# Eight experts on one core: the chunks of the two kinds of expert issued as a pipeline

## The chip, the cores and the metric

The kernel runs on one core of a Trainium2 chip. TensorE (PE) multiplies, VectorE (DVE) and ScalarE (ACT) do the elementwise work, and SyncE (SP) issues nearly all transfers from HBM. The metric is the device time of one execution in microseconds; lower is better.

## The reference

A two-layer latent-diffusion backbone over 256 latent tokens and 256 context tokens of width 1024. Each layer is a modulated norm, one input projection split over four mixers, an output projection, and a channel mixer. The channel mixer of the second layer, the part that the change touches, is top-2 of 8 SwiGLU experts:

```python
def moe_swiglu(h, router, w1, w3, w2):
    logits = (h @ router).astype(jnp.float32)
    top_v, top_i = lax.top_k(logits, TOP_K)
    probs = jax.nn.softmax(top_v, axis=-1)
    combine = jnp.sum(jax.nn.one_hot(top_i, N_EXPERTS, dtype=jnp.float32) * probs[..., None], axis=-2).astype(h.dtype)
    out = jnp.zeros_like(h)
    for e in range(N_EXPERTS):
        out = out + combine[..., e:e + 1] * swiglu(h, w1[e], w3[e], w2[e])
    return out
```

Each expert has w1 and w3 of 1024 x 3584 and w2 of 3584 x 1024, all in float32: 44 MB an expert, 352 MB for the eight.

## The kernel before

**Tiling.** Everything up to the router takes the first half of the run; then come the experts, in `moe`. The kernel sorts the eight experts by load. Three are *heavy* (up to 128 tokens each) and five are *light* (up to 64 tokens). An expert's 3584 inner columns are cut into seven *chunks* of 512. A chunk needs six *units* of weights of 1 MB each: two of w1, two of w3, two of w2.

**A heavy chunk** works in two float32r parts for each operand. Each unit is *split*: ACT rounds a half to float32r (line 145), DVE takes the rest (line 146), and the raw buffer is then free. `moe_first` multiplies by w1 and w3 (three products for each block of 128 rows, lines 176, 181, 182), takes Silu of the first on ACT and multiplies by the second on DVE. `moe_second` *turns* the rows g on PE (transposes, line 1104), copies them into G1 and G2 (lines 1107, 1108), and multiplies by w2 into the two banks `y0`, `y1`.

**A light chunk** multiplies the raw float32 weights as they land, two products side by side in the array. `light_first` is line 1139 (with Silu in 1144 and the multiply in 1145), `light_second` turns the rows (1153, 1155) and multiplies by w2 into `yl` (1163).

**Order.** `moe` makes one list of (expert, chunk) steps: four light chunks first, then both kinds interleaved evenly. A step does the first products of its chunk and then the turning and the second products of the chunk *before* it, of whatever kind that was. After an expert's last chunk, `scatter` or `light_scatter` scales its result, turns it back to tokens and adds it to the residual (`put`, lines 1187 to 1190). The tokens of later experts are gathered in steps (line 1058) between the weight units of the chunks, one step a unit.

**What sets the order on the engines.** A scheduler orders each engine's instructions by priority on a modelled timeline; `keep` pins an instruction behind the one issued before it on its engine. The products of the experts are pinned, the transposes that turn the rows are not. Loads and splits carry a high priority (`ahead`), so they are issued as early as their buffers allow.

**Buffers.** Ten raw buffers of 1 MB are used in turn by both kinds (`load_raw`, line 119), and four halves each for the two split parts, which is two units. Three further buffers serve once at the start, and four units of the first light chunk lie in the split buffers that no heavy chunk uses yet.

Of the kernel before, what the change touches and what calls it, by code (L numbers as in the profile page):

```python
# [9 lines left out]
F32 = mybir.dt.float32  # L10
# [3 lines left out]
AF = mybir.ActivationFunctionType  # L14
ALU = mybir.AluOpType
# [7 lines left out]
EFF_CH = 7  # L23
NE = 8


NH, CAP, LCAP = 3, 128, 64
# [22 lines left out]
class Net:  # L50
# [1028 lines left out]
    def pt_tile(self):  # L1079
        return self.E.tile([128, 2, 128], F32R, tag="PT", name=self.nm("PT"), bufs=2)  # L1080

    def moe_first(self, src, XE, c, aside=lambda: None):

        nc = self.nc
        hs = []
        for name in ("m_w1", "m_w3"):
            ps = self.bank(tag="mm")
            for kh in range(2):
                w = self.split_unit(src(name, c, kh))
                for kk in range(4):  # L1090
                    k = 4 * kh + kk
                    self.mm3(ps, (XE[:, 0, k], XE[:, 1, k]), w(512 * kk, 512 * kk + 512), k == 0, k == 7)
                aside()
            hs.append(ps)
        g = self.t2()
        nc.scalar.activation(g, hs[0], AF.Silu)
        nc.vector.tensor_tensor(g, g, hs[1], op=ALU.mult)
        return g

    def moe_second(self, src, c, g, y, last=False):  # L1100
        nc, E = self.nc, self.E
        pt = self.bank((128, 4, 128), tag="sm")
        for j in range(4):
            nc.tensor.transpose(pt[:, j], g[:, 128 * j:128 * j + 128], self.ident)  # L1104
        G1 = E.tile([128, 4, 128], F32R, tag="G1", name=self.nm("G1"), bufs=2)
        G2 = E.tile([128, 4, 128], F32R, tag="G2", name=self.nm("G2"), bufs=2)
        nc.scalar.copy(G1, pt)  # L1107
        nc.vector.tensor_tensor(G2, pt, G1.bitcast(F32), op=ALU.subtract)
        for hb in range(2):
            self.cut = 2 if last and hb + self.ncut > 1 else 1  # L1110
            w = self.split_unit(src("m_w2", c, hb))
            self.cut = 1
            for b in range(2):
                j = 2 * hb + b
                for hf in range(2):
                    o = 1024 * b + 512 * hf
                    self.mm3(y[hf], (G1[:, j], G2[:, j]), w(o, o + 512), c == 0 and j == 0, c == EFF_CH - 1 and j == 3)

    def raw_unit(self, src):
        if self.halves:  # L1120
# [3 lines left out]
            raw = self.load_raw(src)  # L1124
        return lambda a, b: raw[:, a:b]

    def light_first(self, src, XL, c, aside=lambda: None):

        nc = self.nc
        hs = []  # L1130
        for name in ("m_w1", "m_w3"):
            ps = self.bank((128, 256), tag="mm")
            for kh in range(2):
                w = self.raw_unit(src(name, c, kh))
                for kk in range(4):
                    k = 4 * kh + kk
                    for b in range(2):
                        o = 512 * kk + 256 * b
                        self.keep(nc.tensor.matmul(ps[64 * b:64 * b + 64], XL[:, k], w(o, o + 256), start=(k == 0),  # L1139
                                                   stop=(k == 7), tile_position=(0, 64 * b)))  # L1140
                aside()
            hs.append(ps)
        g = self.t2()[:, :256]
        nc.scalar.activation(g, hs[0], AF.Silu)
        nc.vector.tensor_tensor(g, g, hs[1], op=ALU.mult)  # L1145
        return g

    def light_second(self, src, c, g, y, last=False):

        nc, E = self.nc, self.E  # L1150
        pt = self.bank((128, 2, 128), tag="sm")
        for j in range(2):
            nc.tensor.transpose(pt[:, j], g[:, 128 * j:128 * j + 128], self.ident)  # L1153
        G = E.tile([128, 2, 128], F32, tag="GL", name=self.nm("GL"), bufs=2)
        nc.scalar.copy(G, pt)  # L1155
        for hb in range(2):
            self.cut = 2 if last and hb + self.ncut > 1 else 1
            w = self.raw_unit(src("m_w2", c, hb))
            self.cut = 1
            for b in range(2):  # L1160
                for hf in range(2):
                    o = 1024 * b + 512 * hf
                    self.keep(nc.tensor.matmul(y[64 * hf:64 * hf + 64], G[:, b, 64 * hb:64 * hb + 64], w(o, o + 512),  # L1163
                                               start=(c == 0 and hb == b == 0), stop=(c == EFF_CH - 1 and hb == b == 1),
                                               tile_position=(0, 64 * hf)))

    def scatter(self, PT, y, cmb):

# [39 lines left out]

    def moe(self):
        nc, E = self.nc, self.E  # L1210
        XE, PT = {}, {}

        def tables(i):
            tabs = (self.pos, self.sel, self.comb) if i == 0 else self.placed
# [19 lines left out]
        def turn(i, P, Q=None):  # L1234
            if Q is None:
                self.turned(PT[i], [P[:, t, :128] for t in range(2)])
            else:
                self.turned(PT[i].rearrange("p t h c -> p (t h) c"), [x for t in range(2) for x in (P[:, t, 128:], Q[:, t])])

        def gather(i, j):  # L1240

            P = E.tile([128, 2, 256], F32R, tag="P", name=self.nm("P"), bufs=1)
            if i:
                heavy(i, P)
            Q = light(j, P)
            yield from self.gather(P[:, :, 0 if i else 128:192], XE.get(i), XE[j])
            if i:
                turn(i, P)
            turn(j, P, Q)

        def begin():
            yield from gather(None, 0)
            self.weights()
            self.by_load()
            yield
            yield from gather(1, NH + 1)

        def run(gen, n=1000):
            for _ in range(n):
                if next(gen, self) is self:  # L1260
                    break

        big = lambda i: 0 < i <= NH
        pend, side, late = None, begin(), iter(())
        run(side, 9)
        hs, ls = ([(i, c) for i in p for c in range(EFF_CH)] for p in (range(1, NH + 1), [0, *range(NH + 1, NE)]))

        n = self.lead
        rest = [((k + 0.5) / len(q), x) for q in (hs, ls[n:]) for k, x in enumerate(q)]
        steps = ls[:n] + [x for _, x in sorted(rest, key=lambda a: a[0])]  # L1270
        more = {(NH + k, 2): (k + 1 if k < NH else None, NH + k + 1) for k in range(1, NE - NH - 1)}
        y = {}
        for i, c in steps:
            e = self.ids[i]
            if i == 0:
                src = lambda name, c, j: self.d[name][0, c, j]
            else:
                src = lambda name, c, j, e=e: self.d[name][bass.ds(e, 1), c, j].rearrange("a p c -> (a p) c")
            if i == 0 and c == 4:
                self.gdma = False  # L1280
                gf = self.O.tile([128, 2, 1024], F32, tag="gf", name="gf")
                self.g2, self.fg = self.gate(2, 0, gf[:, 0]), gf[:, 1]
                nc.scalar.dma_start(self.fg, self.d["fng"])
            if c == 0 and i not in PT:
                run(side)
            g = (self.moe_first if big(i) else self.light_first)(src, XE[i], c, lambda: run(side, self.gstep))
            run(late)
            if pend is not None:
                late = self.moe_finish(*pend, PT, tables)
                run(late, 1)  # L1290
            if c == 0:
                y[big(i)] = self.ys() if big(i) else self.bank(tag="yl")
            pend = (i, src, c, g, y[big(i)])
            if (i, c) in more:
                run(side)
                side = gather(*more[i, c])
        run(late)
        run(self.moe_finish(*pend, PT, tables))

    def moe_finish(self, i, src, c, g, y, PT, tables):  # L1300
        last = i == NE - 1 and c == EFF_CH - 1
        big = 0 < i <= NH
        (self.moe_second if big else self.light_second)(src, c, g, y, last)
        if c == EFF_CH - 1:
            yield from (self.scatter if big else self.light_scatter)(PT[i], y, tables(i)[2])

    def moe_rest(self):

        nc, E, V = self.nc, self.E, self.nc.vector
# [4 lines left out]
        with self.tc.If(over > 0):  # L1314
            with self.tc.For_i(0, NE, 1) as e:
# [3 lines left out]
                for name, a in (("pos", self.pos[:, :2]), ("sel", self.sel), ("comb", self.comb),  # L1319
                                ("slots", self.slots)):  # L1320
                    q = self.tmp
# [8 lines left out]
                XE, PT = self.xe_tile(), self.pt_tile()  # L1330
# [3 lines left out]
                src = lambda name, c, i: self.d[name][bass.ds(e, 1), c, i].rearrange("a p c -> (a p) c")  # L1334
                y = self.ys()
                for c in range(EFF_CH):
                    g = self.moe_first(src, XE, c)
                    self.moe_second(src, c, g, y)
                for _ in self.scatter(PT, y, cmb):
                    pass  # L1340
                V.tensor_scalar(cur, cur, -1.0, None, op0=ALU.add)
# [318 lines left out]
```

## Time and profile before

| | |
|---|---|
| median of 3 runs | 1692.35 us (1692.28 to 1695.18) |
| profiled execution | 1697.85 us, its span 1696.1 us |
| granted TensorE clock, mean | 0.984 |
| PE busy | 1624.5 us, 96% of the span |
| weight loads on PE | 1187.7 us, 70% |
| DVE / ACT busy | 961.3 us, 57% / 685.0 us, 40% |
| HBM read | 478.86 MB |

A busy share is an average over stages with different limits, and matmuls are pipelined, so a busy PE is not a PE at its peak. The experts' weights are moved from 795 us to about 1664 us of the span; that stretch is the one to read. The profiled execution is 5.5 us longer than the median of the timed runs.

### The profile page before, as it was taken

To read this page: it belongs to the slowest core of one execution; us is meant where nothing else is said; L and a number is where in the kernel's file an instruction comes from. 1 tells how busy PE (TensorE), PEld (TensorE's weight loads), DVE (VectorE), ACT (ScalarE), POOL (GpSimd) and SP (SyncE) were. 2 spreads that over 40 slices of the span, in tenths; PEclk is the share of its full clock that TensorE was granted. 3 is DMA by queue.
4 is the path that set the end of the run, shared out by engine and by line. 5 is a ranking of instruction groups with operands and counts; after the bars stand their busy time and mean duration, and the time that the engine had idled before them with its cause. 6 is when DMAs were issued, how large, how long until landed. Compare 5 with 4: busy or idle time off the path is not lost. (4 is left out here: it accounts for less than half of the span.)

```text
span 1696.1 us, 23693 instructions
## 1 busy us (share of the span) xinstructions
PE 1624.5 (96%) x9333; PEld 1187.7 (70%) x9333; DVE 961.3 (57%) x1455; ACT 685.0 (40%) x1086; POOL 35.4 (2%) x46
## 2 busy tenths in 40 slices
PE   6999999999999999999899999999999999999996
PEld 3878799887787878999656566656665666665663
DVE  3769655568565688588424454446463535363354
ACT  4654244422222226665424334334453343343342
POOL 1000000000000031000000000000000000000000
PEclk8999999999999999999799999999999999999998
DMA  8544451444443542325799999999999999999993
GB/s 348 196 174 147 154 190 51 174 148 177 163 183 127 203 167 101 125 76 203 312 394 420 419 419 410 384 413 400 420 415 415 420 406 387 411 419 419 420 419 132
DMA packets 69031, 481.56 MB, mean 284 GB/s; under 512 B 8064, under 2 KB 8192, under 8 KB 12336
## 3 DMA queue, kind: packets, MB, share of 16 engines
q1 hardware_dynamic: 68480, 479.43, 71.5%
q8 instruction: 75, 1.23, 0.3%
q10 hardware_dynamic: 432, 0.54, 0.1%
q14 instruction: 44, 0.36, 0.1%
HBM read 478.86 MB, written 1.08 MB: 283 GB/s over the span
## 5 line engine op out<-in xcount | busy, mean ns | idle before, releaser
L146 DVE TENSOR_TENSOR s<-raw,s 128x1024 fp32r<-128x1024 f32 (+1 forms) x376 | 446.4, 1222 | 134.9 <-ACT s L145 134.4
L145 ACT CAST s<-raw 128x1024 fp32r<-128x1024 f32 (+1 forms) x376 | 383.1, 1049 | 270.2 <-PE mm L182 109.3
L176 PE MATMUL mm<-X,s 128*128 128x512 f32 (+1 forms) x672 | 247.4, 369 | 0.0
L181 PE MATMUL mm<-X,s 128*128 128x512 f32 (+1 forms) x672 | 247.3, 368 | 0.0
L182 PE MATMUL mm<-X,s 128*128 128x512 f32 (+1 forms) x672 | 246.0, 368 | 0.0
L1139 PE MATMUL mm<-raw,XL 128*64 128x256 f32 x1808 | 207.5, 381 | 0.0
L1139 PEld LDWEIGHTS mm<-raw,XL 128*64 128x64 f32 x1808 | 127.2, 137 | 71.2 <-issue 12.2
L176 PEld LDWEIGHTS mm<-X,s 128*128 128x128 f32 x672 | 126.6, 188 | 27.7 <-issue 6.7
L181 PEld LDWEIGHTS mm<-X,s 128*128 128x128 f32 x672 | 126.9, 189 | 25.8 <-issue 5.9
L182 PEld LDWEIGHTS mm<-X,s 128*128 128x128 f32 x672 | 126.7, 189 | 23.9 <-issue 3.4
L181 PE MATMUL mm<-s,XE 128*128 128x512 f32 x336 | 138.3, 411 | 4.2 <-DVE s L146 4.2
L176 PE MATMUL mm<-s,XE 128*128 128x512 f32 x336 | 135.7, 404 | 3.0 <-ACT s L145 3.0
L182 PE MATMUL mm<-s,XE 128*128 128x512 f32 x336 | 134.7, 401 | 0.0
L1163 PE MATMUL yl<-raw,GL 128*64 128x512 f32 x456 | 110.3, 604 | 1.0 <-ACT GL L1155 1.0
L1145 DVE TENSOR_TENSOR t<-t,mm 128x256 f32<-128x256 f32 x35 | 14.7, 421 | 170.2 <-PE mm L1139 170.2
L181 PEld LDWEIGHTS mm<-s,XE 128*128 128x128 f32 x336 | 64.4, 192 | 36.4 <-issue 13.8
L176 PE MATMUL mm<-s,X 128*128 128x256 f32 (+1 forms) x304 | 87.3, 289 | 2.0 <-ACT mix L666 2.0
L181 PE MATMUL mm<-s,X 128*128 128x256 f32 (+1 forms) x304 | 86.8, 287 | 0.8 <-DVE s L146 0.8
L182 PE MATMUL mm<-s,X 128*128 128x256 f32 (+1 forms) x304 | 86.0, 288 | 0.0
L176 PEld LDWEIGHTS mm<-s,XE 128*128 128x128 f32 x336 | 64.4, 192 | 23.9 <-ACT s L145 7.5
L181 PE MATMUL y<-s,G 128*128 128x512 f32 x168 | 68.8, 410 | 11.3 <-DVE s L146 11.3
L1107 ACT CAST G<-sm 128x512 fp32r<-128x512 f32 x21 | 12.3, 586 | 160.0 <-PE sm L1104 160.0
(382 smaller groups left out, 2273.9 us busy)
## 6 DMA issues: line engine op xcount, KB each, us to landing
raw<-in_m_w_dram SPq DMA_DIRECT2D x294, 1024.0 KB, 10.0
mraw<-in_mod_w_dram SPq DMA_DIRECT2D x47, 1024.0 KB, 4.8
raw<-in_f_w_dram SPq DMA_DIRECT2D x33, 1024.0 KB, 4.9
mraw<-in_m_w_dram SPq DMA_DIRECT2D x32, 1024.0 KB, 9.8
raw<-in_w_in_dram SPq DMA_DIRECT2D x20, 1024.0 KB, 4.8
raw<-in_w_out_dram SPq DMA_DIRECT2D x8, 1024.0 KB, 5.5
first<-in_m_w_dram SPq DMA_DIRECT2D x8, 512.0 KB, 8.7
once<-in_m_w_dram SPq DMA_DIRECT2D x3, 1024.0 KB, 16.2
```

What stands on the lines that cost most here:

```text
L145: self.last = (nc.scalar.copy(s1[:, :h], r), nc.vector.tensor_tensor(s2[:, :h], r, s1[:, :h].bitcast(F32), op=ALU.subtract))
L146: nc.vector.tensor_tensor(s2[:, :h], r, s1[:, :h].bitcast(F32), op=ALU.subtract))
L176: m = mm(out, a[0], b[0], start=first, stop=False)
L181: self.keep(mm(out, a[0], b[1], start=False, stop=False))
L182: self.keep(mm(out, a[1], b[0], start=False, stop=last))
L1107: nc.scalar.copy(G1, pt)
L1139: self.keep(nc.tensor.matmul(ps[64 * b:64 * b + 64], XL[:, k], w(o, o + 256), start=(k == 0), stop=(k == 7), tile_position=(0, 64 * b)))
L1145: nc.vector.tensor_tensor(g, g, hs[1], op=ALU.mult)
L1163: self.keep(nc.tensor.matmul(y[64 * hf:64 * hf + 64], G[:, b, 64 * hb:64 * hb + 64], w(o, o + 512), start=(c == 0 and hb == b == 0), stop= ...
```

## The change

The products are the same and so are all transfers. What changes is the order in which the steps' parts are issued:

- `moe_second` and `light_second` lose their turning, which becomes `moe_turn` and `light_turn`. Their transposes are now pinned too.
- Light rows are turned after the first product (w1) of the next step, heavy rows at the start of the next heavy step.
- The second products of a heavy chunk are issued between the two first products (w1 and w3) of the next heavy chunk; those of a light chunk ahead of a later light step, or behind it where the next step is light again.
- A light step that is followed by a heavy one loads and splits the heavy chunk's two w1 units (`self.pre`) ahead of its own multiply on DVE, which is pinned behind those splits.
- Gather steps run only in heavy steps, three at a time in three of the four places, and whatever is left runs just before the expert's first step. The gather for the first heavy expert, which ran between the units of the first light chunks, now runs behind the fifth.
- The heavy chunks are drawn forward by a factor of 0.95 in the list, so that the list ends heavy, light, light; before it ended light, heavy, light. The last heavy expert's second products and its scatter now come ahead of the last light chunk.

```diff
     def moe_first(self, src, XE, c, aside=lambda n: None):
...
+        g = self.t2()
+        for n, name in enumerate(("m_w1", "m_w3")):
             ps = self.bank(tag="mm")
             for kh in range(2):
...
+                if n == kh == 1:
+                    nc.vector.tensor_tensor(g, g, ps, op=ALU.mult)
+                elif kh == 1:
+                    nc.scalar.activation(g, ps, AF.Silu)
+                aside(2 * n + kh)
...
+    def moe_turn(self, g):
+
         nc, E = self.nc, self.E
         pt = self.bank((128, 4, 128), tag="sm")
         for j in range(4):
-            nc.tensor.transpose(pt[:, j], g[:, 128 * j:128 * j + 128], self.ident)
+            self.keep(nc.tensor.transpose(pt[:, j], g[:, 128 * j:128 * j + 128], self.ident))
         G1 = E.tile([128, 4, 128], F32R, tag="G1", name=self.nm("G1"), bufs=2)
         G2 = E.tile([128, 4, 128], F32R, tag="G2", name=self.nm("G2"), bufs=2)
         nc.scalar.copy(G1, pt)
         nc.vector.tensor_tensor(G2, pt, G1.bitcast(F32), op=ALU.subtract)
+        return G1, G2
...
+                aside(2 * n + kh)
+            if n == 0:
+                nc.scalar.activation(g, ps, AF.Silu)
+            else:
+                self.keep(nc.vector.tensor_tensor(g, g, ps, op=ALU.mult))
         return g
...
-        rest = [((k + 0.5) / len(q), x) for q in (hs, ls[n:]) for k, x in enumerate(q)]
+        rest = [((k + 0.5) / len(q) * f, x) for q, f in ((hs, 0.95), (ls[n:], 1)) for k, x in enumerate(q)]
...
+        def heavy_aside(n):
+            if n == 1:
+                turns(False)
+                puts()
+                second(True)
             else:
+                run(side, 3)
...
+            def light_aside(n):
+                if n == 1:
+                    turns(False)
+                if n == 3 and big(after[0]):
+
+                    if after[0] not in ready:
+                        puts()
+                        run(side)
+                    src = source(after[0])
+                    self.pre = [self.split_unit(src("m_w1", after[1], kh)) for kh in range(2)]
+
+            if kind:
+                turns(True)
+                g[i, c] = self.moe_first(source(i), XE[i], c, heavy_aside)
+            else:
+                second(False)
+                g[i, c] = self.light_first(source(i), XE[i], c, light_aside)
+                if not big(after[0]):
+                    second(False)
+            todo[kind].append((i, c))
+            if not kind and todo[True] and not any(big(x) for x, _ in steps[m:]):
+                turns(True)
+                second(True, aside=lambda: turns(False))
+                puts()
...
+        turns(False)
+        second(False, last=True)
+        puts()
```

## Rows read from the trace of the kernel before

**Rows 1.** The page: GB/s moved in 40 slices of 42.4 us.
```profile
GB/s 348 196 174 147 154 190 51 174 148 177 163 183 127 203 167 101 125 76 203 312 394 420 419 419 410 384 413 400 420 415 415 420 406 387 411 419 419 420 419 132
```

**Rows 2.** Windows by stage: busy us of each engine, PE clock, DMA share, GB/s.
```profile
833.00:846.00 13.00, 13.00 (x97) 7.71 (x94) 3.96 (x14) 4.74 (x11) 0.00 (x0) 0.90 0.44 181
846.00:900.00 54.00, 52.80 (x361) 29.61 (x362) 13.10 (x26) 14.70 (x27) 0.00 (x0) 1.00 0.98 388
900.00:1030.00 130.00, 125.35 (x705) 80.72 (x704) 61.69 (x69) 51.17 (x69) 0.00 (x0) 0.99 1.01 419
1030.00:1450.00 420.00, 401.81 (x2279) 261.49 (x2278) 206.45 (x240) 172.26 (x231) 0.00 (x0) 0.99 1.00 406
1450.00:1660.00 210.00, 202.24 (x1138) 129.27 (x1138) 97.01 (x97) 80.42 (x97) 0.00 (x0) 1.00 1.01 419
...
900.00:1660.00 760.00, 729.39 (x4117) 471.48 (x4117) 365.16 (x404) 303.86 (x396) 0.00 (x0) 0.99 1.01 412
```

**Rows 3.** The same view in windows of 10 us: a dip, and the stream's end.
```profile
1060.00:1070.00 10.00, 10.00 (x46) 5.49 (x46) 2.70 (x3) 1.43 (x3) 0.00 (x0) 1.00 0.91 322
...
1660.00:1670.00 10.00, 8.94 (x70) 5.92 (x66) 4.17 (x6) 4.53 (x6) 0.00 (x0) 1.00 0.47 186
```

**Rows 4.** Line 119, its loads, issue to landing: windows 1050 to 1075, 1600 to 1625.
```profile
DMA to landing us min/median/max: 5.5/5.8/5.9
...
DMA to landing us min/median/max: 13.5/15.3/16.5
```

**Rows 5.** Waits of SP's own queue, 900 to 1660: us, times, longest.
```profile
SPq L119 <- DVE s L146: 256.7, 111, 4.8
SPq L119 <- PE mm L1139: 189.4, 116, 7.1
```

**Rows 6.** Waits of PE, 900 to 1660: us in total, times, longest.
```profile
PE sm L1153 <- DVE t L1145: 11.9, 20, 0.6
PE y L181 <- DVE s L146: 10.8, 15, 1.7
PE mm L181 <- DVE s L146: 4.2, 4, 2.3
```

**Rows 7.** The chain that ended last: a light chunk's pieces, a heavy turning (start, us).
```profile
1440.31 0.59 PE sm L1104 x4
...
1453.60 7.08 PE mm L1139 x64
1460.78 0.43 DVE t L1145
1461.26 0.44 PE sm L1153 x2
1461.69 3.58 PE yl L1163 x16
```

**Rows 8.** Timeline: two heavy products, one behind the other (start, us).
```profile
1466.01 0.39 PE L176 MATMUL mm<-s,XE 128*128 128x512 f32 x1
...
1466.24 0.40 PE L181 MATMUL mm<-s,XE 128*128 128x512 f32 x1
```

**Rows 9.** Groups by line, 860 to the end: DVE's splits (busy, mean ns, idle before).
```profile
L146 DVE TENSOR_TENSOR s<-raw,s 128x1024 fp32r<-128x1024 f32 x252 | 295.8, 1222 | 74.2 <-ACT s L145 73.9
```

**Rows 10.** A window of 1 us behind PE's longest wait (columns of Rows 2).
```profile
970.00:971.00 1.00, 1.00 (x4) 0.81 (x3) 1.00 (x2) 0.34 (x1) 0.00 (x0) 0.50 1.08 451
```

**Rows 11.** Timelines of SP and of PE in the first light chunk.
```profile
845.95 0.33 SPq L119 DMA_DIRECT2D mraw<-in_m_w_dram  x1
...
843.34 0.69 PE L1058 MATMUL sm<-P,H 128*128 128x192 f32 x4
```

**Rows 12.** Timeline of the end.
```profile
1675.77 1.94 PE L1163 MATMUL yl<-raw,GL 128*64 128x512 f32 x8
...
1680.90 0.62 ACT L1199 CAST Y<-t 128x512 fp32r<-128x512 f32 x1 [3.68 <-PE mm L1188]
...
1689.94 0.69 DVE L1574 TENSOR_TENSOR out<-out,gf 128x512 f32<-128x512 f32 x1
```

More of the change, by code (lines that the diff above doesn't have):

```diff
@@ L1080, in pt_tile, with moe_first @@
         return self.E.tile([128, 2, 128], F32R, tag="PT", name=self.nm("PT"), bufs=2)
-    def moe_first(self, src, XE, c, aside=lambda: None):
+    def moe_first(self, src, XE, c, aside=lambda n: None):
         nc = self.nc
-        hs = []
-        for name in ("m_w1", "m_w3"):
+        g = self.t2()
+        for n, name in enumerate(("m_w1", "m_w3")):
             ps = self.bank(tag="mm")
@@ L1092, in moe_first @@
                     self.mm3(ps, (XE[:, 0, k], XE[:, 1, k]), w(512 * kk, 512 * kk + 512), k == 0, k == 7)
[L1093 to L1097, printed above, removed]
+                if n == kh == 1:
[3 more added lines that the diff above has]
+                aside(2 * n + kh)
         return g
-    def moe_second(self, src, c, g, y, last=False):
+    def moe_turn(self, g):
         nc, E = self.nc, self.E
@@ L1108, in moe_second @@
         nc.vector.tensor_tensor(G2, pt, G1.bitcast(F32), op=ALU.subtract)
+        return G1, G2
+    def moe_second(self, src, c, G, y, last=False, aside=lambda: None):
+        G1, G2 = G
         for hb in range(2):
@@ L1117, in moe_second @@
                     self.mm3(y[hf], (G1[:, j], G2[:, j]), w(o, o + 512), c == 0 and j == 0, c == EFF_CH - 1 and j == 3)
+            if hb == 0:
+                aside()
     def raw_unit(self, src):
@@ L1125, in raw_unit, with light_first @@
         return lambda a, b: raw[:, a:b]
-    def light_first(self, src, XL, c, aside=lambda: None):
+    def light_first(self, src, XL, c, aside=lambda n: None):
         nc = self.nc
-        hs = []
-        for name in ("m_w1", "m_w3"):
+        g = self.t2()[:, :256]
+        for n, name in enumerate(("m_w1", "m_w3")):
             ps = self.bank((128, 256), tag="mm")
@@ L1140, in light_first, with light_turn, light_second @@
                                                    stop=(k == 7), tile_position=(0, 64 * b)))
[L1141 to L1145, printed above, removed]
-        return g
-    def light_second(self, src, c, g, y, last=False):
-        nc, E = self.nc, self.E
+                aside(2 * n + kh)
[3 more added lines that the diff above has]
+                self.keep(nc.vector.tensor_tensor(g, g, ps, op=ALU.mult))
+        return g
+    def light_turn(self, g):
+        nc = self.nc
         pt = self.bank((128, 2, 128), tag="sm")
         for j in range(2):
-            nc.tensor.transpose(pt[:, j], g[:, 128 * j:128 * j + 128], self.ident)
-        G = E.tile([128, 2, 128], F32, tag="GL", name=self.nm("GL"), bufs=2)
+            self.keep(nc.tensor.transpose(pt[:, j], g[:, 128 * j:128 * j + 128], self.ident))
+        G = self.E.tile([128, 2, 128], F32, tag="GL", name=self.nm("GL"), bufs=2)
         nc.scalar.copy(G, pt)
+        return G
+    def light_second(self, src, c, G, y, last=False):
         for hb in range(2):
@@ L1162, in light_second @@
                     o = 1024 * b + 512 * hf
-                    self.keep(nc.tensor.matmul(y[64 * hf:64 * hf + 64], G[:, b, 64 * hb:64 * hb + 64], w(o, o + 512),
-                                               start=(c == 0 and hb == b == 0), stop=(c == EFF_CH - 1 and hb == b == 1),
-                                               tile_position=(0, 64 * hf)))
+                    self.keep(self.nc.tensor.matmul(y[64 * hf:64 * hf + 64], G[:, b, 64 * hb:64 * hb + 64], w(o, o + 512),
+                                                    start=(c == 0 and hb == b == 0),
+                                                    stop=(c == EFF_CH - 1 and hb == b == 1), tile_position=(0, 64 * hf)))
     def scatter(self, PT, y, cmb):
@@ L1210, in moe @@
         nc, E = self.nc, self.E
-        XE, PT = {}, {}
+        XE, PT, ready = {}, {}, set()
         def tables(i):
@@ L1249, in gather @@
             turn(j, P, Q)
+            ready.update((i, j))
         def begin():
@@ L1263, in moe @@
         big = lambda i: 0 < i <= NH
-        pend, side, late = None, begin(), iter(())
+        side = begin()
         run(side, 9)
@@ L1268, in moe, with source, turns, puts @@
         n = self.lead
-        rest = [((k + 0.5) / len(q), x) for q in (hs, ls[n:]) for k, x in enumerate(q)]
+        rest = [((k + 0.5) / len(q) * f, x) for q, f in ((hs, 0.95), (ls[n:], 1)) for k, x in enumerate(q)]
         steps = ls[:n] + [x for _, x in sorted(rest, key=lambda a: a[0])]
         more = {(NH + k, 2): (k + 1 if k < NH else None, NH + k + 1) for k in range(1, NE - NH - 1)}
-        y = {}
-        for i, c in steps:
-            e = self.ids[i]
+        def source(i):
             if i == 0:
-                src = lambda name, c, j: self.d[name][0, c, j]
-            else:
-                src = lambda name, c, j, e=e: self.d[name][bass.ds(e, 1), c, j].rearrange("a p c -> (a p) c")
+                return lambda name, c, j: self.d[name][0, c, j]
+            return lambda name, c, j, e=self.ids[i]: self.d[name][bass.ds(e, 1), c, j].rearrange("a p c -> (a p) c")
+        y, g, G, late = {}, {}, {}, []
+        todo = {True: [], False: []}
+        def turns(kind):
+            for x in todo[kind]:
+                if x in g:
+                    G[x] = (self.moe_turn if kind else self.light_turn)(g.pop(x))
+        def puts():
+            while late:
+                run(late.pop(0))
+        def second(kind, **kw):
+            while todo[kind] and todo[kind][0] in G:
+                i, c = x = todo[kind].pop(0)
+                if c == 0:
+                    y[i] = self.ys() if kind else self.bank(tag="yl")
+                (self.moe_second if kind else self.light_second)(source(i), c, G.pop(x), y[i], **kw)
+                if c == EFF_CH - 1:
+                    late.append((self.scatter if kind else self.light_scatter)(PT[i], y[i], tables(i)[2]))
+                    run(late[-1], 1)
+        def heavy_aside(n):
[3 more added lines that the diff above has]
+                second(True)
+            else:
+                run(side, 3)
+        for m, (i, c) in enumerate(steps):
+            kind = big(i)
             if i == 0 and c == 4:
@@ L1283, in moe @@
                 nc.scalar.dma_start(self.fg, self.d["fng"])
-            if c == 0 and i not in PT:
+            if c == 0 and i not in ready:
+                puts()
                 run(side)
[L1286 to L1293, printed above, removed]
+            after = steps[m + 1] if m + 1 < len(steps) else (0, 0)
+            def light_aside(n):
[20 more added lines that the diff above has]
+                puts()
             if (i, c) in more:
+                puts()
                 run(side)
                 side = gather(*more[i, c])
[L1297 to L1305, printed above, removed]
+        turns(False)
+        second(False, last=True)
+        puts()
     def moe_rest(self):
@@ L1337, in moe_rest @@
                     g = self.moe_first(src, XE, c)
-                    self.moe_second(src, c, g, y)
+                    self.moe_second(src, c, self.moe_turn(g), y)
                 for _ in self.scatter(PT, y, cmb):
```

## The prediction

> **What bounds the kernel now.** I read the page's slices first. From the 22nd slice to the 39th the rate stands at 400 to 420 GB/s, but for two of 384 and 387 [rows 1]. Cut into stages, the experts run at 419 GB/s from 900 to 1030 us and again from 1450 to 1660 us, with a DMA share of 1.01, and at 406 GB/s between [rows 2]. So 419 GB/s is the ceiling that this trace shows, and one unit (1.0486 MB) takes 1.0486 / 419 = 2.50 us, a chunk of six 15.0 us.
>
> Next, whether PE is slower or faster than that. A light chunk takes 7.08 + 3.58 + 0.44 = 11.1 us [rows 7]. A heavy product follows the one before by 0.23 us [rows 8], so 72 of them and the turning (0.59) take 17.2 us. Over the whole mixture, gathers and scatters included, PE is busy for 729.4 of the 760 us from 900 to 1660, and idle for 30.6 us. In the same time 412 x 760 = 313.1 MB moved, which at 419 GB/s would have taken 747.3 us [rows 2]. This is the main finding: the transfers need 747, PE's work needs 729, and the stage took 760. Neither is the bound by itself; PE's idle 30.6 us, added to its work, overtake the transfers.
>
> The coupling is the ten raw buffers. SP waits for a unit's release by a split (DVE) or a light product (PE), not for the bus [rows 5]. How many loads stand in the queue is read from the time to landing: 15.3 us is six units ahead, 5.8 us about two [rows 4]. Where it nears two, the stream thins out: 322 GB/s at 1060 us [rows 3].
>
> Last, the end. The window from 1660 moved 186 GB/s for 10 us [rows 3], which is 4.4 us at the ceiling, so the last unit landed at about T = 1664.4. The last product ends at 1677.7 [rows 12], 13.3 us later, since PE was behind; the span ends at 1696.1, 31.7 us after T.
>
> **The change, part by part.**
>
> *1. PE's waits.* The turning of light rows waits for the multiply on DVE 20 times (11.9 us), the second heavy products wait 15 times for a split (10.8 us), and the first heavy products at least 4 times (4.2 us) [rows 6]. With the rows turned in the middle of the next step, the multiply (0.43 us) has a whole product of PE's to lie beside: half of 7.08 us in a light step, and 24 x 0.23 = 5.6 us in a heavy one. With w1 split ahead, PE finds two units ready when it comes from a light step. These are 26.9 of the 30.6 us. They aren't worth 26.9, as the transfers need 747.3 of the 760 us: at most 12.7 us can come from this stretch (stage by stage, 13 / 419 x 420 = 13.0 us, all from 1030 to 1450). PE has 747.3 - 729.4 = 17.9 us for whatever waits remain. Drawing the heavy chunks forward costs a part of this: 29.4 light chunks beside 21 heavy ones, where there were 31, are 326 + 361 = 687 us of PE against 50.4 x 15 = 756, where it was 705 against 780; the ratio rises from 0.904 to 0.909, about 4 us. If no wait remained, I would take 12.7. If half of them came back (15 us), PE's slack would be gone and the gain about 11; if all came back, 0. I take 11, bounds 0 and 13.
>
> *2. The start.* Until 846 us SP waits for the first unit that shares a ring buffer [rows 11]; the stream has stood since 833 (181 GB/s), and 846 to 900 runs at 388 [rows 2], which is 31 / 419 x 54 = 4.0 us lost. Moving the gather out from between the light units takes four pieces of about 0.69 us off PE ahead of that release [rows 11], 2.8 us. Against it the same gather, eight blocks, now comes in one go behind the fifth light step, 5.5 us of PE and more if it waits for its copies; by then ten buffers are to be filled, 25 us of transfers, so most of it is covered. Bounds 0 and 6.8; I take 2, nearer the lower one since the covered stop comes when the queue may be short.
>
> *3. The end.* Before, the last heavy expert's second products (24 x 0.23 = 5.6 us), part of its scatter and the last light chunk's second products (3.6) all lay behind the last light chunk's first ones. Now the heavy ones come a chunk earlier. With the stream ending at T, w3 of the last light chunk lands 5 us before T (two units follow), PE takes its last unit (7.08 / 4 = 1.8 us), multiplies and turns (0.43 + 0.44 and the copy, some 1.4 us in all) and does the second products (3.6): 5.0 - 1.8 - 1.4 - 3.6 = -1.8, so PE ends 1.8 us after T if it isn't behind. The heavy scatter and the light chunk before it put it some 3 us more behind, by an estimate from the same pieces: eight units (20 us) land after the heavy w2, and PE has about 2.8 + 4 + 3.6 + 7.1 + 1.4 + 3.6 = 22.5 us for what comes with them. I take 4 in place of 13.3, a gain of 9. Behind it the cast of the last result into Y waited 3.68 us on ACT for the heavy scatter's product [rows 12]; about 1.7 us of that lie behind its own input, which is ready at 1679.2, and go. Sum 11; bounds 7 (PE 7 us behind, and Y gains 1) and 13 (1.8 behind).
>
> *4. What is added.* No product, split or transfer is. The pinned multiply of a light step now stands behind four split instructions of 1.22 us [rows 9] and the landing of two units. I cost that at nothing: PE has 5.6 us of heavy w1 products ahead of the turning, and the multiply needs only the last split plus 0.43. Queued behind it on DVE are the heavy chunk's later splits, which wait for PE to free the split buffers anyway. Two heavy g rows instead of one may lie in the four `t2` buffers; a scatter (two more) then waits, at most for a few steps of 0.7 us, five times. SP issues the same units in the order in which they are used, so no load stands behind one that is used later.
>
> The sum: 11 + 2 + 11 = 24 us off the profiled execution's 1697.85, so 1673.9 there; the median runs are 0.32% shorter, so **1668 us**. With every bound at its best it is 33 us less (1659), with the waits of part 1 only partly gone (6) and the low bounds of the rest, 13 less (1679).
>
> **A rule on the ceiling.** The sum goes by 419 GB/s, which no window of a stage exceeds [rows 2]. [...]
>
> **The rivals.**
>
> *PE stays the bound.* The waits come back in another form: ACT and DVE work in order, and with the queue longer they stand at splits whose units haven't landed; or PE, now waiting for units, loses its clock. [...] A light unit would leave PE idle for 2.50 - 1.77 = 0.73 us. That speaks for it; against it, the many waits of 0.6 us before [rows 6] left the clock of 900 to 1660 at 0.99 [rows 2], and a PE that has fallen behind finds its units landed and no longer waits. Then only the end is shorter, by 10 us: 1692.35 - 10 = **1682**. [...]
>
> *Slower, by a late split.* A split for a later heavy unit is put ahead of the rows' multiply or of the G copies on DVE, so that PE's pinned transposes stand until it is done. A pinned transpose lets nothing pass. The price is two splits, 2.44 us [rows 9], for each of the 21 heavy steps at the turning, and as much again at the second products: 102 us, of which the 30.6 us that PE loses now and the end's 10 are taken off: 61 more, **1753** in full; at one stand a step, 51 - 41 = 10 more, **1702**. It decides from 41 / 21 = 2.0 us a step. Against it: heavy rows are turned a whole step after they are made.
>
> *No change.* The scheduler reorders by its own modelled times, and the order written may come out as now; then PE's 30.6 us and the end stay, 1692. But the pinned transposes and the moved heavy chunk at the end don't depend on that.
>
> **How the numbers follow.** Likeliest (parts 1 to 3 as costed, 1659 to 1679): 0.58. PE stays the bound, 1679 to 1688: 0.22. No change, within 0.2% (3.4 us, about what a measurement of this kernel can tell): 0.07. Slower: 0.13. Faster is 0.58 + 0.22 = 0.80. The range holds the likeliest case and most of the second: 1658 to 1686.
>
> **What would show it.** Right: 1030 to 1450 at 417 to 420 GB/s, time to landing at 12 us or more nearly throughout, PE waiting for DMA rather than for DVE, the last unit landed at about 1651 and the last product some 4 us later. Wrong: PE transposes or second products that wait for ACT or DVE for longer than before, a clock under 0.97 in the experts' stage, or a stretch under 400 GB/s where time to landing falls below 6 us.

## The result, and the profile after

The changed kernel is slower: 1717.28 us median, 1.0133 of the kernel before, 95% interval [1.0119, 1.0147]. The profiled execution's span is 1715.3 us, 19.2 us more than before. The forecast was 1668 us.

The stages first, in the view of windows with the columns of [rows 2], kernel after:

```profile
846.00:900.00 54.00, 51.47 (x321) 31.82 (x318) 17.19 (x36) 18.52 (x36) 0.00 (x0) 0.91 0.96 393
900.00:1030.00 130.00, 122.66 (x700) 81.02 (x698) 59.39 (x63) 48.93 (x62) 0.00 (x0) 0.98 0.99 408
1030.00:1450.00 420.00, 392.81 (x2257) 266.67 (x2257) 202.06 (x238) 171.54 (x233) 0.00 (x0) 0.97 0.97 397
1450.00:1660.00 210.00, 197.05 (x1069) 132.09 (x1069) 100.14 (x101) 80.47 (x97) 0.00 (x0) 0.97 0.99 403
...
900.00:1660.00 760.00, 712.51 (x4022) 479.77 (x4022) 361.59 (x400) 300.95 (x390) 0.00 (x0) 0.97 0.98 401
1680.00:1690.00 10.00, 9.41 (x58) 4.78 (x59) 3.88 (x6) 0.44 (x1) 0.00 (x0) 1.00 0.08 29
```

No stage holds the 419 GB/s that two of them held before [rows 2]. PE is idle for 760 - 712.5 = 47.5 us instead of 30.6, and its mean clock has gone from 0.99 to 0.97. The last unit lands at about 1680 + 29 x 10 / 419 = 1680.7, 16.3 us later than before; the other 2.9 us are in the end.

What PE waits for, 900 to 1660 us (us in total, times, longest), kernel after; the rows for [rows 6]:

```profile
PE mm L176 <- ACT s L145: 24.3, 15, 1.6
PE mm L181 <- DVE s L146: 9.5, 16, 0.8
PE yl L1173 <- DVE t L1208: 6.0, 4, 1.5
```

And the first of these rows in the kernel before:

```profile
PE mm L176 <- ACT s L145: 3.0, 2, 1.6
```

Two of the waits of before are gone as forecast: in this stretch neither the turning of the light rows nor the second heavy products stand among PE's waits. In their place stands a wait that was rare before: the *first* products of a heavy chunk stand for 1.6 us until ACT has cast w1, at 15 steps where there were two, and then for up to 0.8 more until DVE has split it. Together that is 33.8 us, against 7.2 before. These are the units that the change splits ahead. The third row, a light chunk's second products behind an expert's scatter, is new too, and all kernels below that are made from the changed one have it.

One such step, in the timelines of PE and of ACT (start, us, engine, line, instruction, idle before and what ended it), kernel after:

```profile
1098.16 3.62 PE L1146 MATMUL mm<-raw,XL 128*64 128x256 f32 x32
1101.71 0.66 PE L1105 MATMUL sm<-ident,t 128*128 128x128 f32 x4
1103.98 0.49 PE L176 MATMUL mm<-s,XE 128*128 128x512 f32 x1 [1.62 <-ACT s L145]
1105.24 0.50 PE L181 MATMUL mm<-s,XE 128*128 128x512 f32 x1 [0.77 <-DVE s L146]
...
1106.83 0.63 PE L176 MATMUL mm<-s,XE 128*128 128x512 f32 x1
1107.25 0.63 PE L181 MATMUL mm<-s,XE 128*128 128x512 f32 x1
```

```profile
1098.37 0.38 ACT L1150 ACTIVATE t<-mm 128x256 f32<-128x256 f32 x1 [15.02 <-PE mm L1146]
1102.40 0.59 ACT L1108 CAST G<-sm 128x512 fp32r<-128x512 f32 x1 [3.65 <-PE sm L1105]
1102.88 3.89 ACT L145 CAST s<-raw 128x1024 fp32r<-128x1024 f32 x4
```

ACT is idle for 3.65 us while PE works through the light chunk, then copies the turned heavy rows (G, line 1108), and only then casts the four halves of w1. The copy stands ahead of the casts in ACT's queue, and no cast starts before it. PE turns the heavy rows at the end of the light step, so the copy can't come before 1102.4, and what stands behind it waits. Of the 20 heavy steps that begin with a turning, the copy stands ahead of all four casts of w1 in 17 of the kernel after, behind two of them in one and behind all four in two.

And the granted clock of the same step, in windows of 1 us, kernel after:

```profile
1105.00:1106.00 1.00, 0.76 (x3) 0.66 (x4) 1.00 (x2) 1.00 (x2) 0.00 (x0) 1.00 0.99 410
1107.00:1108.00 1.00, 1.00 (x4) 0.81 (x3) 1.00 (x2) 0.94 (x1) 0.00 (x0) 0.50 1.01 418
1110.00:1111.00 1.00, 1.00 (x6) 0.81 (x5) 0.36 (x2) 0.67 (x1) 0.00 (x0) 1.00 1.01 418
```

Behind the two waits PE runs at a granted clock of 0.50 for some 3.4 us; products that follow each other by 0.23 us at 1.00 then take 0.43.

The fall doesn't come every time. In windows of 1 us from 900 to 1640 there are 12 such stretches of 3.4 us: nine behind the waits for w1, three behind waits in a gather or a scatter. Six of the 15 waits for w1 are followed by none. One of the six is at 955.81 us, with waits of 1.62 and 0.76 us; the windows behind it, kernel after:

```profile
956.00:960.00 4.00, 3.24 (x14) 2.39 (x14) 4.00 (x4) 3.65 (x5) 0.00 (x0) 1.00 1.01 420
960.00:964.00 4.00, 4.00 (x20) 3.23 (x19) 4.00 (x5) 3.30 (x4) 0.00 (x0) 1.00 1.02 420
```

What decides between the two isn't shown here. Added up over 185 windows of 4 us from 900 to 1640 us, twice the length times (1 - clock), PE spends 40.9 us at half clock, against 10.3 before. Half of the difference, 15.3 us, is PE time lost, about as much as the 16.9 us of idle time that came on top.

### The profile page after: what moved, and what is told of

It reads as the page before. It is cut to its first block, busy times and chain, and to the rows that moved or that the text cites. A ratio compares the mean times of both kernels' runs of the same rounds, so it can differ in the third digit from the quotient of the medians.

```text
span 1715.3 us, 23719 instructions
## 1 busy us (share of the span) xinstructions
PE 1623.0 (95%) x9333; PEld 1206.8 (70%) x9333; DVE 960.1 (56%) x1455; ACT 684.7 (40%) x1086; POOL 35.4 (2%) x46
## 5 line engine op out<-in xcount | busy, mean ns | idle before, releaser
L146 DVE TENSOR_TENSOR s<-raw,s 128x1024 fp32r<-128x1024 f32 (+1 forms) x350 | 419.1, 1222 | 111.9 <-ACT s L145 110.0
L145 ACT CAST s<-raw 128x1024 fp32r<-128x1024 f32 (+1 forms) x350 | 357.9, 1050 | 275.3 <-PE mm L182 109.0
L1146 PE MATMUL mm<-raw,XL 128*64 128x256 f32 x1952 | 218.4, 380 | 0.0
L1146 PEld LDWEIGHTS mm<-raw,XL 128*64 128x64 f32 x1952 | 139.0, 137 | 81.2 <-issue 15.9
L176 PE MATMUL mm<-s,XE 128*128 128x512 f32 x336 | 141.2, 420 | 24.3 <-ACT s L145 24.3
L181 PE MATMUL mm<-s,XE 128*128 128x512 f32 x336 | 141.8, 422 | 9.5 <-DVE s L146 9.5
L1150 ACT ACTIVATE t<-mm 128x256 f32<-128x256 f32 x35 | 13.4, 383 | 316.6 <-PE mm L1146 316.6
L182 PE MATMUL mm<-s,XE 128*128 128x512 f32 x336 | 139.0, 414 | 0.0
L1109 DVE TENSOR_TENSOR G<-sm,G 128x512 fp32r<-128x512 f32 x21 | 14.5, 691 | 168.7 <-ACT G L1108 168.7
L176 PEld LDWEIGHTS mm<-s,XE 128*128 128x128 f32 x336 | 67.1, 200 | 43.5 <-ACT s L145 27.8
L181 PEld LDWEIGHTS mm<-s,XE 128*128 128x128 f32 x336 | 67.3, 200 | 30.5 <-DVE s L146 15.3
```

Source lines behind the costliest of these rows:

```text
L145: self.last = (nc.scalar.copy(s1[:, :h], r), nc.vector.tensor_tensor(s2[:, :h], r, s1[:, :h].bitcast(F32), op=ALU.subtract))
L146: nc.vector.tensor_tensor(s2[:, :h], r, s1[:, :h].bitcast(F32), op=ALU.subtract))
L176: m = mm(out, a[0], b[0], start=first, stop=False)
L181: self.keep(mm(out, a[0], b[1], start=False, stop=False))
L182: self.keep(mm(out, a[1], b[0], start=False, stop=last))
L1150: nc.scalar.activation(g, ps, AF.Silu)
```

## The experiments

Theory A: the order of ACT's and DVE's queues (the copies of the turned rows ahead of the splits) makes the wait. Theory B: the new order of PE itself costs the time, with the second products in the middle, the transposes pinned and the scatters inside. Theory C, beside A: the clock that falls behind the wait is a cost of its own.

**Turning inside the first product.** The heavy rows are turned behind the first w1 unit.

```diff
+            if n == 0:
+                turns(True)
             if n == 1:
                 turns(False)
...
             if kind:
-                turns(True)
                 g[i, c] = self.moe_first(source(i), XE[i], c, heavy_aside)
```

> The heavy rows are turned behind the first w1 unit of the next heavy step, no longer ahead of it; nothing else changes. Queue order (theory A: in the changed kernel the copy of the turned heavy rows stands ahead of the splits of w1 on ACT and DVE, so PE waits 1.6 + 0.8 us at 15 heavy steps, and the clock falls behind it): the 33.8 us of waits of the first heavy products go but for a few us, the clock of the experts' stage returns from 0.97 to 0.99, and the time falls by 34 us or more, to 1665 to 1685 us, where the transfers bound it. Pinned order (theory B: second products in the middle, the pinned transposes and scatters in PE's order cost the time): less than 10 us, 1707 us or more.

1685.07 us, 0.9940 of before [0.9923, 0.9956]. PE's waits for first products, 900 to 1660, turned inside:

```profile
PE mm L176 <- ACT s L145: 3.4, 4, 1.7
PE mm L181 <- DVE s L146: 3.4, 7, 0.8
```

They fell from 33.8 us to 6.8. Theory A; the time is just above the upper end of what it gave, and the fall is 32 us where 34 or more was expected.

**Copies pinned.** PE's order stays.

```diff
-        nc.scalar.copy(G1, pt)
-        nc.vector.tensor_tensor(G2, pt, G1.bitcast(F32), op=ALU.subtract)
+        self.keep(nc.scalar.copy(G1, pt))
+        self.keep(nc.vector.tensor_tensor(G2, pt, G1.bitcast(F32), op=ALU.subtract))
```

> PE's order stays as in the changed kernel; only the two copies of the turned heavy rows (to G1 on ACT, to G2 on DVE) are pinned behind what was issued before them on their engine, the splits of w1 among it. Theory A: as much as turning inside, 1665 to 1690 us, and the waits of first heavy products on ACT and DVE fall from 33.8 us to under 8. Theory B: PE's order is the same, so 1707 us or more.

1681.41 us, 0.9911 [0.9894, 0.9928]: 36 us less than the changed kernel, and faster than the kernel before. The same step as above, timelines of ACT and of PE, copies pinned:

```profile
1091.05 0.38 ACT L1150 ACTIVATE t<-mm 128x256 f32<-128x256 f32 x1 [15.02 <-PE mm L1146]
1091.33 4.06 ACT L145 CAST s<-raw 128x1024 fp32r<-128x1024 f32 x4
1095.30 0.58 ACT L1108 CAST G<-sm 128x512 fp32r<-128x512 f32 x1
```

```profile
1094.38 0.66 PE L1105 MATMUL sm<-ident,t 128*128 128x128 f32 x4
1094.79 0.48 PE L176 MATMUL mm<-s,XE 128*128 128x512 f32 x1
1095.11 0.39 PE L181 MATMUL mm<-s,XE 128*128 128x512 f32 x1
```

The casts now run while PE is still in the light chunk, so their data had landed; the first product follows the turning without a wait. The stages, and PE's waits from 900 to 1660, copies pinned:

```profile
846.00:900.00 54.00, 51.46 (x330) 31.41 (x327) 15.63 (x34) 16.95 (x33) 0.00 (x0) 0.91 0.98 401
900.00:1030.00 130.00, 125.62 (x728) 83.51 (x726) 65.19 (x70) 54.13 (x69) 0.00 (x0) 1.00 0.99 404
1030.00:1450.00 420.00, 407.79 (x2371) 275.45 (x2371) 211.39 (x247) 177.34 (x239) 0.00 (x0) 0.99 1.01 416
1450.00:1640.00 190.00, 178.37 (x1016) 118.19 (x1013) 87.70 (x89) 75.87 (x91) 0.00 (x0) 0.98 1.01 419
```

```profile
PE mm L181 <- DVE s L146: 5.0, 7, 1.4
PE mm L176 <- ACT s L145: 4.2, 6, 1.1
...
PE mm L1146 <- DMA raw<-in_m_w_dram: 2.3, 7, 0.5
```

The wait has fallen from 33.8 to 9.2 us (under 8 was expected), half-clock time from 40.9 to 13.8, and the stream is nearly full from 1030 us on. Theory B is out as the cause of the loss: PE's order is that of the changed kernel.

**No splits ahead**, without and with the pin. The loads and splits of w1 in the light step are left out:

```diff
-                    src = source(after[0])
-                    self.pre = [self.split_unit(src("m_w1", after[1], kh)) for kh in range(2)]
```

> The changed kernel without the load and split of the heavy w1 units ahead of the light multiply. Theory A: the splits come behind the turning in any case, so the waits stay at 25 to 45 us and the time within 8 us of the changed kernel, 1709 to 1725 us. Rival (the light multiply pinned behind the splits is what costs): below 1700 us.

> The kernel with both copies pinned (1681.4 us), without the load and split of w1 ahead of the light multiply. Queue order (theory A): with nothing traced ahead to be pinned behind, the splits stand behind the copy again, the waits of the first heavy products return to 25 us or more, and the time to 1705 to 1718 us: the pin and the splits ahead are worth something only together. Rival (the pin itself is what helps): below 1692 us.

1711.68 us, 1.0090 [1.0073, 1.0107], and with the pin 1712.18 us, 1.0093 [1.0076, 1.0110]. PE's waits, 900 to 1660, pinned and nothing ahead:

```profile
PE mm L176 <- ACT s L145: 24.3, 15, 1.6
PE mm L181 <- DVE s L146: 9.1, 13, 0.9
```

The same 24.3 us as in the changed kernel. So the splits ahead, as the change issues them, gain nothing: without them the kernel is even 0.4% faster (1.0090 against 1.0133), for a reason that no run here separates. Together with the pin they make 0.9911. Neither half is worth anything alone.

**Which queue.** The pin on one of the two copies only.

```diff
-        nc.scalar.copy(G1, pt)
+        self.keep(nc.scalar.copy(G1, pt))
```

> The changed kernel with only the copy to G1, on ACT, pinned behind the splits; on DVE the scheduler is free. Theory A: ACT's place is what matters, since DVE's split follows ACT's cast: waits of first heavy products under 12 us, time within 4 us of the kernel with both pinned, 1678 to 1686 us. Rival (DVE's order matters as much): 1695 us or more.

> The changed kernel with only the copy to G2, on DVE, pinned behind the splits; on ACT the copy to G1 still stands ahead of them. Theory A: PE still waits for the transposes, the copy to G1, the cast and the split in a row, 1.6 + 0.8 us at 15 steps; the time stays within 6 us of the changed kernel, 1708 to 1722 us. Rival (DVE's order matters as much): below 1700 us.

With ACT's copy pinned 1682.18 us, 0.9918 [0.9902, 0.9935]; with DVE's alone 1723.32 us, 1.0157 [1.0140, 1.0174], 1.3 us above what was expected, and the wait is 26.7 us at 17 steps. Pinning ACT's copy is enough, and pinning DVE's alone gains nothing. The kernel with ACT's copy pinned can't quite separate the two: with ACT's copy later, the scheduler put DVE's behind the splits as well.

**The gap filled.** Ten transposes of a constant, read by nobody, stand at the start of 18 heavy steps, in 17 of them behind a turning.

```diff
             if kind:
                 turns(True)
+                if len(hdone) not in (7, 8, 20):
+                    pd = self.bank((128, 4, 128), tag="sm")
+                    for j in range(10):
+                        self.keep(nc.tensor.transpose(pd[:, j % 4], self.ident, self.ident))
+                hdone.append(i)
```

> The changed kernel with ten transposes more on PE (of a constant, 0.15 us each, read by nobody) behind the turning of the heavy rows in 18 of the 21 heavy steps, where the copy stands ahead of the splits: PE works for 1.5 us of the wait and the wait itself is as long as before. Theory C (the granted clock, which is half for 41 us of 900 to 1640 against 10 before, is a cost of its own behind the wait): the half-clock time falls to 20 us or less, and the time by 6 to 12 us, to 1705 to 1711 us. Rival (the waits alone cost the time): no fall, 1715 us or more.

1705.67 us, 1.0061 [1.0044, 1.0078]: 0.7% less, some 12 us, with 180 transposes (23.7 us of PE's busy time) *more*. The timeline of PE at the step shown above, gap filled:

```profile
1099.78 0.66 PE L1105 MATMUL sm<-ident,t 128*128 128x128 f32 x4
1100.28 1.25 PE L1347 MATMUL sm<-ident 128*128 128x128 f32 x10
1102.06 0.49 PE L176 MATMUL mm<-s,XE 128*128 128x512 f32 x1 [0.53 <-ACT s L145]
1103.32 0.50 PE L181 MATMUL mm<-s,XE 128*128 128x512 f32 x1 [0.77 <-DVE s L146]
1103.66 0.39 PE L182 MATMUL mm<-s,XE 128*128 128x512 f32 x1
1103.89 0.40 PE L176 MATMUL mm<-s,XE 128*128 128x512 f32 x1
```

From the turning to line 181's product it is 3.54 us here and 3.53 in the kernel after: at this step what PE waits for is as late as before. But the products behind it follow each other by 0.23 us, not 0.43, and the half-clock time from 900 to 1640 is 6.9 us. The edit didn't meet every wait: 11 steps have the filler and a rest of the wait, and at none of them does the clock fall; three have the wait of 1.62 us without a filler, and the two falls that are left (1178 and 1625 us) stand behind two of these. At one more step, 956 us, two casts came ahead of the copy, so that there the wait of 2.4 us went too; some 2 of the 12 us are that, by an estimate from its length. Theory C holds: most of the gain is the clock's part of the loss, had back by useless work.

**The list alone.** The kernel before with the factor of 0.95, and the pinned kernel with the factor back at 1.

```diff
-        rest = [((k + 0.5) / len(q), x) for q in (hs, ls[n:]) for k, x in enumerate(q)]
+        rest = [((k + 0.5) / len(q) * f, x) for q, f in ((hs, 0.95), (ls[n:], 1)) for k, x in enumerate(q)]
```

> The kernel before with nothing but the list's factor of 0.95, so that it ends heavy, light, light. Forecast of the prediction's third part: PE's lag behind the last transfer falls and the time with it, by 4 to 10 us, 1682 to 1689 us. Rival: PE is behind by the depth of the raw buffers whatever the order, and the time stays within 3 us of 1692.

> The kernel with the copies pinned, and the list's factor back at 1, so that it ends light, heavy, light with the heavy chunks spread evenly. Forecast of the prediction: the heavy second products and their scatter lie behind the last transfer again; PE's lag grows by some 5 us or more and the time by 4 to 12 us. Rival: the factor is worth nothing, as it was on the kernel before: within 3 us.

The first: 1697.86 us, 1.0010 [1.0000, 1.0021]. The gain forecast for the end didn't come: its stream ends at 1665.5 and the last product at 1678.9, 13.4 us behind, as before (13.3). The second: 1685.70 us, 0.9929 [0.9910, 0.9947] against 0.9911, within the uncertainty of either, where 4 to 12 us were expected. So the list by itself is worth little, less than I had put on it.

**The gather at the start, and the last scatter**, on the pinned kernel, each alone and both:

```diff
             def light_aside(n):
+                if m < 4:
+                    run(side, 1)
                 if n == 1:
                     turns(False)
+                    if m == len(steps) - 1:
+                        puts()
...
                 second(True, aside=lambda: turns(False))
-                puts()
```

> The kernel with the copies pinned (1681.4 us), and the gather for the first heavy expert spread again over the units of the first four light chunks, one step behind each, as in the kernel before. Theory A2 (the gather in one go behind the fifth light step stops PE for 10 us with the buffers full, so the stream stops: 390 GB/s at 880 to 900, 322 at 900 to 920 us): both windows return to 410 GB/s or more, and the time falls by 3 to 6 us. Rival (PE's work is only moved, and the stream stops earlier for it): within 2 us of the kernel with the copies pinned.

> The kernel with the copies pinned, and the last heavy expert's products of its scatter moved from ahead of the last light chunk into its middle. Theory: those products stand in PE's order waiting for DVE and ACT for about 3 us while the stream runs out, so PE ends 8.8 us behind the last transfer; moved, that falls to 5 or 6 and the time by 2 to 4 us. Rival: DVE's adds to the residual are only shifted into the end, no change within 1.5 us.

> Both of the two changes above on the kernel with the copies pinned: the gains add, 5 to 9 us below it, 1672 to 1677 us. Rival: the stream was the bound and either gain is given back, within 3 us of it.

0.9892 [0.9875, 0.9908], 0.9891 [0.9872, 0.9909], and both 0.9887 [0.9869, 0.9906], 1677.51 us: the fastest kernel here, though the three can't be told apart from each other, nor clearly from the pinned one (0.9911). So the gains expected of them, 3 to 6, 2 to 4 and 5 to 9 us, aren't shown by the times. What the gather's place did is seen in the windows. With the gather spread, then with both:

```profile
846.00:900.00 54.00, 54.00 (x366) 32.00 (x363) 15.48 (x28) 16.79 (x30) 0.00 (x0) 1.00 1.00 402
900.00:1030.00 130.00, 125.62 (x730) 83.59 (x729) 66.54 (x74) 56.75 (x74) 0.00 (x0) 1.00 1.01 419
```

```profile
900.00:1640.00 740.00, 709.86 (x4094) 474.84 (x4092) 362.67 (x406) 305.15 (x397) 0.00 (x0) 0.99 1.01 418
1640.00:1650.00 10.00, 10.00 (x64) 5.02 (x62) 4.49 (x7) 1.49 (x3) 0.00 (x0) 1.00 0.91 369
1650.00:1660.00 10.00, 6.95 (x46) 2.87 (x42) 2.03 (x4) 0.84 (x2) 0.00 (x0) 1.00 0.04 16
```

The 404 GB/s of 900 to 1030 are 419 again, and with both edits the stream runs at 418 GB/s to its end at 1640 + 8.8 + 0.4 = 1649.2 us. The prediction had put the last unit at about 1651. With the last scatter moved inside and nothing else, the last product ends 1662.4 - 1655.0 = 7.4 us behind the last unit, where it was 8.7; 5 or 6 was expected.

## Why the prediction was wrong, point by point

**What bounds the kernel** was read rightly: no stage of any kernel here ran above 419 GB/s, and the one with both edits holds 418 from 900 to 1640 us.

**Part 1 failed at one sentence**: "With w1 split ahead, PE finds two units ready when it comes from a light step." It took the order in which the change writes the splits for the order in which ACT meets them. Of the 26.9 us of waits that it meant to remove, 22.7 did go: those of the light turning and of the second heavy products. Those of the first heavy products, which it counted at 4.2 us and which were 7.2 with ACT's row, grew to 33.8, with 30.6 us more at half clock.

With the pin, the part comes out at the size costed: of the 13.0 us lost in 1030 to 1450, (419 - 416) / 419 x 420 = 3.0 are left, a gain of 10 where 11 was forecast. That is in part luck. From 900 to 1640 PE is idle for 740 - 711.8 = 28.2 us in the pinned kernel, against 30.6 before, and the prediction gave 0 if all waits came back. The idle time lies elsewhere: 12.2 us instead of 18.2 in 1030 to 1450, where the stream had been short, and 11.6 instead of 7.8 in 1450 to 1640, where it is full. That the shift makes the gain is an argument; no run separates it.

**Part 4 failed with it.** It costed the moved turning at nothing, and looked only at what stands behind the light *multiply*. It left out that the turning's own copies are instructions on ACT and DVE, whose input PE makes at the end of the light step. What the queue holds behind them can't be ahead any more: 24.3 us of waits for ACT and 9.5 for DVE.

**Part 2 had the wrong sign.** 846 to 900 gained (401 - 388) / 419 x 54 = 1.7 us in the pinned kernel, but 900 to 1030 lost (419 - 404) / 419 x 130 = 4.7: the gather in one go holds PE from 882 to 893 us, no weights are multiplied in that time, and the stream falls to 322 GB/s from 900 to 920. Spread, it is back at 419. Sum -3, forecast +2 with bounds 0 and 6.8.

**Part 3 was sized too high.** In the pinned kernel the last product ends 1663.9 - 1655.2 = 8.7 us behind the last unit, not 4, and behind it 16.2 us follow, where 16.7 were forecast; the end gains 31.7 - 24.9 = 6.8 us of 11. In the changed kernel itself PE was 18 us behind, and the end lost 2.9.

**The rivals.** The slower one had copies and splits in view, but DVE in place of ACT and the order the wrong way round: it put a split ahead of the copies, and what happened was a copy ahead of the splits. Its point of decision, 2.0 us a heavy step, was met: 33.8 us of waits and 15.3 us of clock are 2.3 us for each of the 21. It had 0.13. The one in which PE loses its clock named the cost, but tied it to waits for transfers, and I let it off since a late PE finds its units landed; in 900 to 1660 us of the kernel after, none of PE's waits is for a transfer. Most of the waits behind which the clock fell in the kernel after were for a queue, nine of the 12. In the kernel before, the clock stood at 0.50 behind PE's longest wait, 2.3 us for DVE [rows 6, rows 10]. In the kernel after, the fall came behind waits for ACT and DVE of 1.62 and at most 0.77 us, and not each time, but at nine of 15 steps.

Theory A explains the loss and the filled gap shows the clock's share of it. What stays open: the idle and the clock time together are 32.2 us more than before in 900 to 1640, the span grew by 19.2; where the other 13 were given back wasn't separated.

## What to carry to other kernels

In these runs an instruction was ahead only if everything in front of it in its engine's queue was ahead too: with the copy in front, ACT's casts of w1 began at 1102.88 us, after 3.65 us of idle time and the copy; with the copy pinned behind them they began at 1091.33, 3.05 us ahead of the turning. When a step is moved, follow its copies and casts onto the engines that do them, and ask what stands behind them. Splitting ahead and pinning the copies together took the kernel from 1.0090 to 0.9911 of the one before, and neither helped alone, so an edit that disappoints may lack its other half. And price a PE wait with the clock behind it: in the step shown, two waits of 2.4 us in all cost about 1.6 us more in products at half clock, and so at nine steps of 15.

## What the runs showed of the hardware

In the kernel after, PE's clock fell to 0.50 for 3.4 us behind waits that were neither long nor whole, 1.62 us, one product, at most 0.77 us, though only at nine of 15 such places. Single waits of 0.6 us [rows 6], 20 of them before, left the stage at 0.99 [rows 2]. And work that nobody reads, 1.25 us of it in the gap, kept the clock up at all 11 waits where it stood; that kernel takes 1705.67 us against 1717.28, 0.7% less.
